# A decoder layer on one core: the MLA heads' p turned by VectorE and transfers, q, k and v of MLA ahead of both late gate groups, diff heads 5 units apart

## The chip, the core and the metric

The kernel runs on one core of a Trainium2 chip. The metric is the device time of one execution in microseconds (us). The core has TensorE (PE in the profile, with its weight loads as PEld), VectorE (DVE), ScalarE (ACT), GpSimd (POOL) and SyncE (SP). Each has an instruction queue of its own, works it off in order, and waits on semaphores for the others. Transfers between memory and the core's SBUF are issued from SP's and from POOL's queue and carried out by 16 DMA engines.

## The reference: one layer of a hybrid decoder

In float32, for 256 tokens of width 2048:

```
h = LN(ALPHA*x + 0.5*swiglu(x, ffn1));  h = LN(ALPHA*h + mixer(h));  h = LN(ALPHA*h + 0.5*swiglu(h, ffn2))
mixer(h): c_q, c_kv, k_r, dq, dk, dv, gate_mla, gate_diff = columns of h @ w_in      # 512 512 64 1024 1024 1024 2048 2048
  MLA:    q = rms(c_q) @ w_uq, k = rms(c_kv) @ w_uk, v = rms(c_kv) @ w_uv             # 8 heads, 128 + 64 rotary, v 128
          o_mla = per head: softmax(causal(q k' * scale)) v
  diff:   4 heads, two score maps each:  (softmax(s1) - lam * softmax(s2)) v, s with ALiBi and causal mask, then rms
  y = sigmoid(gate_mla) * (o_mla @ w_br_mla) + sigmoid(gate_diff) * (o_diff @ w_br_diff);  return y @ w_out
swiglu(x) = (silu(x @ w_gate) * (x @ w_up)) @ w_down                                   # d_ff 5632
```

The queries are worked in two blocks of 128 rows, the first against 128 keys, the second against 256; so a head's p is a tile of 128 x 384.

## The kernel before

**Products.** Every weight matrix product is split: both sides are taken apart into a high part (`S.copy` to float32r, an ACT cast, L154) and the rest (a DVE subtraction, L155), and three matmuls (L208, L209, L210) make one product. A weight tile of 128 x 1024 comes by a transfer from SP's queue into `raw` or `sraw`, is split into a pair of `wring` tiles (the ring has six pairs), and is used by 12 matmuls of 512 columns. One such tile with its 12 matmuls is a *unit*. The FFNs and the wide projections of the mixer go through a Strassen-like scheme with seven products and shared sums, the rest through `project`.

**Order of the work.** The program is written in the order of the units. All that isn't a weight product is hung in between by `later(n, fn)`: `fn` runs when n more units have been issued (`tick`). So the numbers given to `later` set where on each engine's queue the small work of heads, turns and transfers comes.

**Turning a row tile to columns without PE.** `turn` (L711 on) does it in four steps: DVE's STREAM_TRANSPOSE of 32 x 32 blocks into a `blocks` tile (L715), four POOL transfers of 64 KB to a `turn` buffer in memory (L717), `wait` units later one POOL transfer back into a `turned` tile (L729), and `more` units later the use: an ACT copy into column tiles (`turn_to_cols`, L737) or a split. `cols_proj` and `pair_cols` use this for qT, kT, dqT and dkT.

**Turning p on PE.** `p_cols` (L1100 on) does it for the heads' p: three PE transposes into a PSUM bank (L1103) and an ACT copy into `pt` (L1105).

**The mixer.** First the projections of the two latents, dq, dk, dv and most of the gates. Then, in `mixer`:

- four diff heads, each in four steps by `diff_head`: `scores` (matmuls L1228, then the softmax on DVE and ACT, and p = p1 - lam p2 on DVE, L1235 and L1237), `turn` (L1103, L1105), `values` (L1248 to L1250), `turn2` (four transposes of the output, L1268). Heads are 6 units apart, steps 3.
- the gate group `gate(1, 2)`, with the reads of the normed latents (`c_back`) hung into it,
- q, its rotary part, k and v of MLA from the latents,
- eight MLA heads by `mla_head`: `scores` (L1301, L1303, softmax, p scaled by its sums on DVE, L1307), `turn` (`p_cols`), `values` (L1317, L1318), 2 units apart and 2 units from step to step, hung under `gate(1, 3)` and the diff branch product,
- `gate(1, 3)`, then the branch products, where stored gates come back by POOL transfers (`get_gates`, L1332), and w_out with the second LayerNorm.

**The FFNs.** Towards the end of the gate and up products of each FFN, the turned h is fetched back in quads of 512 rows for the down product; `get_h` does it on POOL's queue (two transfers of 256 KB a quad, L893), `split_h` splits it.

**Buffers.** Small tiles come from pools with a fixed number of places: 6 for `tmp` (st, blocks, turned, qr, rope tiles and so on), 3 for p and pt, 24 for statistics; PSUM has 5 banks for weight products and 3 for the heads. A tile waits until its place's last readers are done, transfers among them.

Of the kernel before, what the change touches and what calls it, by code (L numbers as in the profile page):

```python
# [11 lines left out]
F32 = mybir.dt.float32  # L12
# [47 lines left out]
def layer_kernel(ctx: ExitStack, tc: tile.TileContext, a: dict, out: bass.AP):  # L60
# [42 lines left out]
    def later(n, fn):  # L103
        uid[0] += 1
        heapq.heappush(todo, (step[0] + n, uid[0], fn))
# [746 lines left out]
    def ffn(n, x, wgu, wdn, residual, g, bt, each, first=None, between=None, nxt=None, cols=None, norm=None, pending=None):  # L852
# [7 lines left out]
        def half(c, b, up, gate, wait=0):  # L860
            q = c // 2
            sg = tmp_tile([P, 256], "sg")
            S.activation(sg, gate, AF.Silu)
            if c % 2 == 0:
                hb[b, q] = tmp_tile([P, 512], "hb")
            o = (c % 2) * 256

            def product():
                V.tensor_tensor(out=hb[b, q][:, o:o + 256], in0=up, in1=sg, op=ALU.mult)
            if wait:  # L870
                later(wait, product)
            else:
                product()
            if c % 2 == 1:
                later(12, lambda: put_h(b, q))
# [14 lines left out]
        def get_h(q):  # L890
            raw = got[q] = act_tile([P, 2, 512], F32, "hraw")
            for b in range(2):
                nc.gpsimd.dma_start(raw[:, b, :], hT[q, b])  # L893

        def split_h(q):
            raw = got.pop(q)
# [34 lines left out]
        for p in range(1, KF // 4):  # L931
            if p == KF // 4 - 1:
                for i, q in enumerate((3, 4, 0)):
                    later(3 + 3 * i, lambda q=q: get_h(q))
                later(13, lambda: split_h(3))
                later(16, lambda: split_h(4))
            hy.group(wgu[2 * p], wgu[2 * p + 1],
                     lambda n, b, bank, snap, op, p=p: sum_done(2 * p + n, b, bank, snap, op),
                     1 < p < KF // 4 - 1, p > 1)
# [160 lines left out]
    def p_cols(p):  # L1100
# [4 lines left out]
        S.copy(pt, t[:, 0:384])  # L1105
        return pt

    def mixer(x):
        c_row = [act_tile([P, 1024], F32, "c_row") for _ in range(2)]
        kr_row = [tmp_tile([P, T], "kr_row") for _ in range(2)]  # L1110
# [41 lines left out]
        project(a["wc1"], x, KD, 256, ckv1_done)  # L1152
        project(a["wc2"], x, KD, 320, ckv2_done)

        def cols_proj(w, xx, kt, name, k0=0, more=10):
            dst = act_tile([P, 4, T], F32, name)

            def done(b, bank):
                t = tmp_tile([P, 512], name + "r")
                S.copy(t, bank)  # L1160
                later(1, lambda: turn_to_cols(t, dst, b, 4, more))
            project(w, xx, kt, 512, done, k0)
            return dst
# [3 lines left out]
        def whole(t, bank, snap, op):  # L1167
            if snap is None:
                S.copy(t, bank)
            else:  # L1170
                V.tensor_tensor(out=t, in0=bank, in1=snap, op=op)
# [13 lines left out]
        def pair_cols(w, name):  # L1185
# [10 lines left out]
        dqT = pair_cols(a["wdq"], "dqT")  # L1196
        dkT = pair_cols(a["wdk"], "dkT")
        dv = [act_tile([P, 1024], F32, "dv") for _ in range(2)]
        hy.group(a["wdv"][0], a["wdv"][1], lambda n, b, bank, snap, op: whole(
            dv[b][:, n * 512:(n + 1) * 512], bank, snap, op), False, True)  # L1200
        look(0, 0)

        back = {}

        def c_back(j):
            if j == 0:
                for key, src in turns.items():
                    back[key] = tmp_tile([P, 512], "turned")
                    nc.gpsimd.dma_start(back[key], src)
            if j >= 4:  # L1210
                i, b = divmod(j - 4, 2)
                cn.put(i, b, turned(back[i, b]))

        def gate(i, f, hook=None):
            project((a["wgm"], a["wgd"])[i][f], x, KD, 512, lambda b, bank: keep_gate(i, f, b, bank), hook=hook)

        od = Acts(MH, "od")

# [54 lines left out]

        for h in range(DH):
            for i, f in enumerate(diff_head(h)):
                later(2 + 6 * h + 3 * i + i // 3, f)
        gate(1, 2, c_back)
        qT = [cols_proj(a["wuq"][c], cn, 4, "qT") for c in range(2)]
        qrT = act_tile([P, 4, T], F32, "qrT")

        def qr_done(b, bank):
            t = tmp_tile([P, 512], "qr")
            tv = t.rearrange("p (j h i) -> p j h i", j=2, h=MH)
            rope(tv[:, 0], tv[:, 1], bank, b, MH)
            later(1, lambda: turn_to_cols(t, qrT, b, 4, 10))
        project(a["wuq"][2], cn, 4, 512, qr_done)
        kT = [cols_proj(a["wuk"][c], cn, 4, "kT", 4, 8) for c in range(2)]
        v = [act_tile([P, 1024], F32, "v") for _ in range(2)]
        for c in range(2):
            project(a["wuv"][c], cn, 4, 512, lambda b, bank, c=c: S.copy(v[b][:, c * 512:(c + 1) * 512], bank), 4)  # L1290
# [3 lines left out]
        def mla_head(h):  # L1294
# [14 lines left out]
                st["p"] = p  # L1309

            def turn():
                st["pt"] = p_cols(st["p"])

            def values():
                pt = st["pt"]
# [6 lines left out]

        for h in range(MH):
            for i, f in enumerate(mla_head(h)):
                later(8 + 2 * h + 2 * i, f)
        gates = {}

        def get_gates(f):
# [69 lines left out]
    ffn(1, xq, a["gu1"], a["dn1"], a["x"], a["ln1_g"], a["ln1_b"], keep(0), first_tokens, second_tokens, h1, a["ln1_cols"])  # L1398

    yq = mixer(h1)  # L1400
    h2 = Acts(KD, "h2", (0, 1, 2))
    ln = LayerNorm(1.0, res[0], a["ln2_g"], a["ln2_b"], keep(1), h2, a["ln2_cols"], ((1, 3, 11, 13), ()), 1,
                   (a["ln1_g"], a["ln1_b"]), (2, 7, 14, 21), lambda: yq.made[3, 1])
# [93 lines left out]
```

## Time and profile before

| what | value |
|---|---|
| time, median of 3 runs | 1973.62 us (1973.51 to 1974.14) |
| profiled execution, its own time | 1972.85 us |
| its span | 1971.1 us |
| mean granted TensorE clock | 0.998 |
| PE busy | 1955.1 us, 99% |
| DVE, ACT, POOL busy | 1773.5, 1265.5, 291.0 us |
| PE's share of the chain that ended last | 95% |
| DMA | 485.71 MB, mean 246 GB/s |

The span is the time from the first to the last instruction of the profiled execution; its own time holds what lies around it too. Busy times are sums over an engine's instructions. In a group's row stand the line, engine and operation, the names out<-in and the shapes, the count, the busy time with the mean of one in ns, and the idle time ahead with what ended it. In a timeline a PE matmul's row shows its start and its modelled length; since matmuls are pipelined, the distance of starts tells what one costs (about 0.227 us for one of 512 columns). The windows' rows give busy times and counts by engine, the granted clock, the DMA engines' share and GB/s.

### The profile page before, as it was taken

To read this page: it belongs to the slowest core of one execution; us is meant where nothing else is said; L and a number is where in the kernel's file an instruction comes from. 1 tells how busy PE (TensorE), PEld (TensorE's weight loads), DVE (VectorE), ACT (ScalarE), POOL (GpSimd) and SP (SyncE) were. 2 spreads that over 40 slices of the span, in tenths; PEclk is the share of its full clock that TensorE was granted. 3 is DMA by queue.
4 is the path that set the end of the run, shared out by engine and by line. 5 is a ranking of instruction groups with operands and counts; after the bars stand their busy time and mean duration, and the time that the engine had idled before them with its cause. 6 is when DMAs were issued, how large, how long until landed. Compare 5 with 4: busy or idle time off the path is not lost.

```text
span 1971.1 us, 25747 instructions
## 1 busy us (share of the span) xinstructions
PE 1955.1 (99%) x8784; PEld 1620.0 (82%) x8784; DVE 1773.5 (90%) x2175; ACT 1265.5 (64%) x1650; POOL 291.0 (15%) x503
## 2 busy tenths in 40 slices
PE   9999999999999999999999999999999999999997
PEld 7888888888888898888888888888888888888886
DVE  7999999999998879988976677789999999999986
ACT  6666767676655566666667765556676776665661
POOL 0112111122100010102223120001211112210000
PEclk9999999999999999999999999999999999999999
DMA  8978888777776666767667668578888878786763
GB/s 309 287 227 262 285 270 251 235 216 281 296 235 222 209 218 254 244 224 259 223 198 241 234 216 271 199 263 254 254 263 294 243 243 249 238 321 237 274 234 124
DMA packets 147478, 485.71 MB, mean 246 GB/s; under 512 B 20961, under 2 KB 21009, under 8 KB 147345
## 3 DMA queue, kind: packets, MB, share of 16 engines
q1 hardware_dynamic: 117360, 397.99, 58.2%
q0 software_dynamic: 29984, 86.07, 16.4%
q8 instruction: 69, 1.13, 0.2%
q14 instruction: 65, 0.52, 0.1%
HBM read 455.13 MB, written 28.84 MB: 246 GB/s over the span
## 4 chain that ended last, share of the span: by engine, by line
PE 95%; DVE 2%; DMA 1%; issue 1%; ACT 0%; SPq 0%; DVEq 0%; ACTq 0%
PE mm L209 30%; PE mm L210 30%; PE mm L208 30%; DVE wring L155 1%; PE tr L208 1%; PE tr L210 1%; PE tr L209 1%; DMA sraw<-in_gu_dram 1%; PE tr L671 0%; DVE sraw L428 0%; ACT wring L154 0%; DMA raw<-in_gu_dram 0%; PE tr L1228 0%; PE tr L1301 0%; PE tr L1303 0%
## 5 line engine op out<-in xcount | busy, mean ns | idle before, releaser
L154 ACT CAST wring<-raw 128x1024 fp32r<-128x1024 f32 (+2 forms) x467 | 482.2, 1038 | 296.5 <-PE mm L210 207.2
L155 DVE TENSOR_TENSOR wring<-raw,wring 128x1024 fp32r<-128x1024 f32 (+2 forms) x467 | 559.1, 1206 | 95.4 <-ACT wring L154 92.8
L154 ACT CAST wring<-sraw 128x1024 fp32r<-128x1024 f32 x436 | 454.8, 1054 | 230.2 <-DVE sraw L428 94.2
L155 DVE TENSOR_TENSOR wring<-sraw,wring 128x1024 fp32r<-128x1024 f32 x436 | 523.2, 1228 | 21.6 <-ACT wring L154 18.8
L210 PE MATMUL mm<-wring,h 128*128 128x512 f32 (+2 forms) x1248 | 480.2, 385 | 0.0
L208 PE MATMUL mm<-wring,h 128*128 128x512 f32 (+2 forms) x1248 | 480.2, 385 | 0.0
L209 PE MATMUL mm<-wring,h 128*128 128x512 f32 (+2 forms) x1248 | 479.8, 385 | 0.0
L209 PE MATMUL mm<-wring,xs 128*128 128x512 f32 x776 | 302.2, 389 | 1.3 <-DVE wring L155 1.3
L208 PE MATMUL mm<-wring,xs 128*128 128x512 f32 x776 | 302.2, 389 | 0.0
L210 PE MATMUL mm<-wring,xs 128*128 128x512 f32 x776 | 302.0, 389 | 0.0
L209 PEld LDWEIGHTS mm<-wring,h 128*128 128x128 f32 x1248 | 234.5, 188 | 46.8 <-DVE wring L155 0.7
L210 PEld LDWEIGHTS mm<-wring,h 128*128 128x128 f32 x1248 | 234.5, 188 | 46.5 <-DVE h L155 0.7
L208 PEld LDWEIGHTS mm<-wring,h 128*128 128x128 f32 x1248 | 234.4, 188 | 46.4 <-ACT h L154 0.6
L428 DVE TENSOR_TENSOR sraw<-sraw,sraw 128x1024 f32<-128x1024 f32 x168 | 200.2, 1229 | 3.5 <-DMA sraw<-in_wdv_dram 1.6
L209 PEld LDWEIGHTS mm<-wring,xs 128*128 128x128 f32 x776 | 145.7, 188 | 32.5 <-DVE wring L155 2.3
L208 PEld LDWEIGHTS mm<-wring,xs 128*128 128x128 f32 x776 | 145.7, 188 | 30.1
L210 PEld LDWEIGHTS mm<-wring,xs 128*128 128x128 f32 x776 | 145.7, 188 | 30.0
L717 POOL DMA_DIRECT2D hT<-blocks x176 | 97.1, 562 | 370.0 <-DVE blocks L715 368.2
L208 PE MATMUL mm<-wring,x 128*128 128x512 f32 x336 | 130.8, 390 | 0.8 <-ACT wring L154 0.8
L209 PE MATMUL mm<-wring,x 128*128 128x512 f32 x336 | 131.0, 390 | 0.5 <-DVE wring L155 0.5
L210 PE MATMUL mm<-wring,x 128*128 128x512 f32 x336 | 130.6, 389 | 0.0
L430 POOL DMA_DIRECT2D sraw<-in_gu_dram x40 | 35.6, 900 | 359.4 <-DVE sraw L428 309.0
(307 smaller groups left out, 2289.6 us busy)
## 6 DMA issues: line engine op xcount, KB each, us to landing
sraw<-in_gu_dram SPq DMA_DIRECT2D x160, 512.0 KB, 5.4
raw<-in_gu_dram SPq DMA_DIRECT2D x159, 512.0 KB, 4.7
raw<-in_dn_dram SPq DMA_DIRECT2D x140, 512.0 KB, 4.7
sraw<-in_gu_dram POOLq DMA_DIRECT2D x40, 512.0 KB, 6.9
sraw<-in_dn_dram SPq DMA_DIRECT2D x36, 512.0 KB, 5.6
hraw<-hT POOLq DMA_DIRECT2D x68, 256.0 KB, 6.2
eraw<-in_gu_dram SPq DMA_DIRECT2D x64, 256.0 KB, 6.0
raw<-in_w_out_dram SPq DMA_DIRECT2D x32, 512.0 KB, 4.3
```

The source lines that it names most:

```text
L154: cast[0] = S.copy(hi, src)
L155: lows[0] = V.tensor_tensor(out=lo, in0=src, in1=hi.bitcast(F32), op=ALU.subtract)
L208: PE.matmul(o, xh, wh, start=first, stop=False, skip_group_check=again)
L209: PE.matmul(o, xh, wl, start=False, stop=False, skip_group_check=again)
L210: PE.matmul(o, xl, wh, start=False, stop=last, skip_group_check=again)
L428: last = V.tensor_tensor(out=R[src][i], in0=R[src][i], in1=R[add[1]][i], op=ALU.add)
L430: nc.gpsimd.dma_start(R["12"][s], source("22", s), accum_op=ALU.add)
L717: nc.gpsimd.dma_start(to.rearrange("(g r) (i f) -> i r g f", g=4, i=4)[i], t[32 * i:32 * (i + 1), :].rearrange("r (g f) -> r g f", g=4))
```

## The change: what it does

Five edits of the program, with the same matmuls in all products:

1. `turn_p` takes the place of `p_cols` for the eight MLA heads: a DVE STREAM_TRANSPOSE of p into `pblocks`, one POOL transfer of it to memory (`pturn`), and 2 units later four POOL transfers back into `pt`, one for each 32 partitions, each of 32 x 12 pieces of 32 floats (128 bytes). `pt` now lies in the large pool. The values follow 8 units behind the scores instead of 4.
2. q, its rotary part, k and v of MLA are projected ahead of `gate(1, 2)`; both late gate groups come behind. The reads of the latents (`c_back`) are hung into the dv products instead. Uses of turned q and k come 4 units after their transfer back instead of 10 or 8.
3. Diff heads are 5 units apart instead of 6.
4. The first three quads of h in each FFN are fetched on SP's queue (`get_half`), one half at a time.
5. In the FFN the product of gate and up is written behind a split (`behind_split(3)`), and `narrow_to(6)` is called behind the mixer; neither moves an instruction.

```diff
+        def get_half(q, b):
+            if b == 0:
+                got[q] = act_tile([P, 2, 512], F32, "hraw")
+            with tc.issue_after(fetched[0].ins):
+                nc.sync.dma_start(got[q][:, b, :], hT[q, b])
...
-                    later(3 + 3 * i, lambda q=q: get_h(q))
+                    for b in range(2):
+                        later(1 + 4 * i + 2 * b, lambda q=q, b=b: get_half(q, b))
...
+    def turn_p(p, keep, more):
+
+        t = tmp_tile([P, 384], "pblocks")
+        V.transpose(t, p)
+        to = dram.tile([P, 384], F32, name=nm("pturn"))
+        nc.gpsimd.dma_start(to, t)
+
+        def back():
+            pt = act_tile([P, 384], F32, "pt")
+            for k in range(4):
+                nc.gpsimd.dma_start(pt[32 * k:32 * (k + 1), :].rearrange("f (b i c) -> f b i c", b=3, i=4),
+                                    to.rearrange("(i f) (b k c) -> k f b i c", i=4, b=3, k=4)[k])
+            keep["pt"] = pt
+        later(more, back)
...
-        def cols_proj(w, xx, kt, name, k0=0, more=10):
+        def cols_proj(w, xx, kt, name, k0=0, more=4):
...
+        back = {}
+
+        def c_back():
+            for key, src in turns.items():
+                back[key] = tmp_tile([P, 512], "turned")
+                nc.gpsimd.dma_start(back[key], src)
+        later(6, c_back)
+        for i in range(2):
+            for b in range(2):
+                later(12 + 4 * i + 2 * b, lambda i=i, b=b: cn.put(i, b, turned(back[i, b])))
...
-                later(2 + 6 * h + 3 * i + i // 3, f)
-        gate(1, 2, c_back)
+                later(2 + 5 * h + 3 * i + i // 3, f)
...
-            later(1, lambda: turn_to_cols(t, qrT, b, 4, 10))
+            later(1, lambda: turn_to_cols(t, qrT, b, 4, 4))
...
-        kT = [cols_proj(a["wuk"][c], cn, 4, "kT", 4, 8) for c in range(2)]
+        kT = [cols_proj(a["wuk"][c], cn, 4, "kT", 4, 4) for c in range(2)]
...
-                st["pt"] = p_cols(st["p"])
+                turn_p(st["p"], st, 2)
...
-                later(8 + 2 * h + 2 * i, f)
+                later(10 + 2 * h + (0, 2, 8)[i], f)
+        gate(1, 2)
```

The changed file's lines are moved: `p_cols` is L1111 and L1113 there, the MLA scores L1322 and L1324, values L1338 and L1339, the diff scores L1250 and values L1270, `pblocks` L1119, `pturn` L1121, the reads of `pt` L1126, the stored gates L1199 and L1354. Counted over the program, PE has 24 transposes less, DVE 8 instructions more, ACT 16 less (8 copies of pt and 8 table loads), POOL 28 more (8 + 32 - 12), SP 12 more.

**PE where an MLA head stands among the diff branch's matmuls.** Before, values of one head, the turn of the next, the scores of the one after (mm is a weight product's bank, tr a head's bank):

```order
4916 L210 MATMUL mm_9038<-wring_5085,od_8093 128x512
4917 L1317 MATMUL tr_9045<-pt_8981,v_8362 128x256
4918 L1318 MATMUL tr_9045<-pt_8981,v_8363 128x128
4919 L1103 MATMUL tr_9052<-ident,p_8995 128x128 x3
4920 L1301 MATMUL tr_9058<-kT_8290,qT_8031 128x128
4921 L1303 MATMUL tr_9058<-krT_5345,qrT_8103 128x128
4922 L1301 MATMUL tr_9058<-kT_8290,qT_8031 128x256
4923 L1303 MATMUL tr_9058<-krT_5345,qrT_8103 128x256
4924 L208 MATMUL mm_9014<-wring_116,od_8088 128x512
```

With the change, at the values of head 0:

```order
4804 L210 MATMUL mm_8847<-wring_104,od_8193 128x512
4805 L1338 MATMUL tr_8854<-pt_8747,v_8134 128x256
4806 L1339 MATMUL tr_8854<-pt_8747,v_8135 128x128
4807 L1322 MATMUL tr_8869<-kT_8070,qT_7824 128x128
4808 L1324 MATMUL tr_8869<-krT_5345,qrT_7877 128x128
4809 L1322 MATMUL tr_8869<-kT_8070,qT_7824 128x256
4810 L1324 MATMUL tr_8869<-krT_5345,qrT_7877 128x256
4811 L208 MATMUL mm_8821<-wring_5085,od_8188 128x512
```

The three transposes between values and scores are gone, and the scores are those of the fourth head after.

**POOL over the first MLA heads, with the change** (gates: a gate stored; pturn: a head's p to memory; pt: its reads):

```order
147 L1199 DMA gates<-gate_8559 128x512
148 L1121 DMA pturn_8660<-pblocks_8658 128x384
149 L1126 DMA pt_8747<-pturn_8660 32x12x32 x3
150 L1121 DMA pturn_8725<-pblocks_8723 128x384
151 L1126 DMA pt_8747<-pturn_8660 32x12x32
152 L1199 DMA gates<-gate_8778 128x512
153 L1126 DMA pt_8811<-pturn_8725 32x12x32 x2
154 L1121 DMA pturn_8789<-pblocks_8787 128x384
```

Before, the same stretch had the stored gates followed by their reads alone; now a head's last reads stand behind the next head's write.

**DVE at diff head 1** (st: scaled scores; nmx: the negative maxima that the exponentials need; qr the rotary part of q). Before, behind head 0's norm and output:

```order
1063 L709 SCALAR_TENSOR_TENSOR f_7941<-t_7937,y_7935 128x2
1064 L1261 SCALAR_TENSOR_TENSOR orow_7943<-tr_7919,f_7941,subg 128x256 x2
1065 L1084 SCALAR_TENSOR_TENSOR st_7949<-tr_7946,bias_92 128x384
1066 L1084 SCALAR_TENSOR_TENSOR st_7965<-tr_7962,bias_92 128x384
1067 L1086 TENSOR_REDUCE mx_7951<-st_7949 128x1
1068 L1087 TENSOR_REDUCE mx_7951<-st_7949 128x1
1069 L155 TENSOR_TENSOR wring_103<-raw_8130,wring_102 128x1024
1070 L1089 TENSOR_SCALAR nmx_7954<-mx_7951 128x2
```

With the change:

```order
1062 L155 TENSOR_TENSOR wring_115<-raw_8165,wring_114 128x1024
1063 L715 STREAM_TRANSPOSE blocks_7937<-qr_7920 128x512
1064 L1079 TENSOR_TENSOR ropec_7962<-mm_7927,sincos 128x512
1065 L1080 TENSOR_TENSOR ropes_7963<-mm_7927,sincos 128x512
1066 L1081 TENSOR_TENSOR qr_7961<-ropec_7962,ropes_7963 128x256
1067 L1082 TENSOR_TENSOR qr_7961<-ropes_7963,ropec_7962 128x256
1068 L1092 SCALAR_TENSOR_TENSOR st_7971<-tr_7968,bias_92 128x384
1069 L1092 SCALAR_TENSOR_TENSOR st_7987<-tr_7984,bias_92 128x384
1070 L1094 TENSOR_REDUCE mx_7973<-st_7971 128x1
1071 L1095 TENSOR_REDUCE mx_7973<-st_7971 128x1
1072 L715 STREAM_TRANSPOSE blocks_8009<-qr_7961 128x512
1073 L1097 TENSOR_SCALAR nmx_7976<-mx_7973 128x2
```

The rotary part of q, which came behind this head's p before, now stands ahead of its st, with one block turn, and a second block turn stands ahead of its nmx; head 0's norm comes later.

More of the change, by code (lines that the diff above doesn't have):

```diff
@@ L868, in product @@
             def product():
-                V.tensor_tensor(out=hb[b, q][:, o:o + 256], in0=up, in1=sg, op=ALU.mult)
+                with behind_split(3) if wait else nullcontext():
+                    V.tensor_tensor(out=hb[b, q][:, o:o + 256], in0=up, in1=sg, op=ALU.mult)
             if wait:
@@ L1201, in mixer, with gate @@
         look(0, 0)
[L1203 to L1215, printed above, removed]
+        def gate(i, f):
+            project((a["wgm"], a["wgd"])[i][f], x, KD, 512, lambda b, bank: keep_gate(i, f, b, bank))
         od = Acts(MH, "od")
@@ L1400, in layer_kernel @@
     yq = mixer(h1)
+    narrow_to(6)
     h2 = Acts(KD, "h2", (0, 1, 2))
```

## The prediction

> **What bounds the kernel now.** I read the page first (spans, engines, chain), then the waits of TensorE, then the chain and the timeline around the longest of these waits.
>
> ```profile
> span 1971.1 us, 25747 instructions
> PE 1955.1 (99%) x8784; PEld 1620.0 (82%) x8784; DVE 1773.5 (90%) x2175; ACT 1265.5 (64%) x1650; POOL 291.0 (15%) x503
> ...
> PE 95%; DVE 2%; DMA 1%; issue 1%; ACT 0%; SPq 0%; DVEq 0%; ACTq 0%
> ```
>
> TensorE (PE) is busy for 1955.1 of 1971.1 us and carries 95% of the chain. So the time can fall in two ways only: fewer or shorter PE instructions, or less of the 16 us in which PE does nothing. Of these 16, the waits of PE show what lies inside the run:
>
> ```profile
> engine line waited for: us in total, times, longest us
> PE mm L209 <- DVE wring L155: 1.8, 4, 0.7
> PE tr L1248 <- ACT pt L1105: 1.1, 1, 1.1
> ...
> PE mm L208 <- ACT wring L154: 0.8, 1, 0.8
> PE tr L1103 <- DVE p L1237: 0.2, 1, 0.2
> ```
>
> Only the rows of L1248 and L1103 lie in the part of the mixer that the change rewrites, 1.3 us together. The others belong to the start or to weight splits of the FFNs, whose order stays. The chain around the 1.1 us:
>
> ```profile
> 1068.04 1.05 ACT wring L154
> 1069.12 1.28 ACT L1092
> ...
> 1071.69 4.50 DMA turned<-turn
> ...
> 1076.75 1.04 ACT wring L154
> 1077.79 0.39 ACT pt L1105
> 1078.22 0.70 PE tr L1248 x2
> ```
>
> ScalarE (ACT) stood in its queue on kT, which comes back by a transfer (turned<-turn), behind a 1.28 us table load; the pt copy of the last diff head came after that, so its values (L1248) were late.
>
> **What PE loses: the turns of the MLA heads.** A stretch of PE with one head, and the start of the next:
>
> ```profile
> 1118.25 0.39 PE L210 MATMUL mm<-wring,od 128*128 128x512 f32 x1
> 1118.47 0.59 PE L1317 MATMUL tr<-pt,v 128*128 128x256 f32 x2
> ...
> 1119.12 0.49 PE L1103 MATMUL tr<-ident,p 128*128 128x128 f32 x3
> 1119.45 0.39 PE L1301 MATMUL tr<-kT,qT 128*128 128x128 f32 x2
> ...
> 1120.58 0.58 PE L208 MATMUL mm<-wring,od 128*128 128x512 f32 x1
> 1121.00 0.39 PE L209 MATMUL mm<-wring,od 128*128 128x512 f32 x1
> ...
> 1126.24 0.59 PE L1317 MATMUL tr<-pt,v 128*128 128x256 f32 x2
> ```
>
> By starts, three transposes take 1119.45 - 1119.12 = 0.33 us, and a weight matmul 1118.47 - 1118.25 = 0.22 to 0.23. Eight heads: 8 x 0.33 = 2.6 us less. Against it, the first weight matmul behind such a group takes 1121.00 - 1120.58 = 0.42, so 0.19 more than the others. Values now stand 8 units behind the scores instead of 4, and with the diff heads 5 units apart the small matmuls fall into more separate groups: in the order of the change PE goes from weight matmuls to small ones 39 times in this part, before 35 times. Four more entries at 0.11 to 0.25 (0.19 on leaving, a few hundredths on entering) give back 0.4 to 1.0. Net -1.6 to -2.2; I take -1.6, the cautious end, since with the group in another place a weight load can miss its cover too.
>
> **The waits that go.** The values of a diff head now follow its turn by 5.4 to 8 us of PE work instead of 1.6 to 3.3, and the kT transfers lie behind other work than before, so the 1.1 of L1248 and the 0.2 of L1103 go, and some 0.1 to 0.2 of restart with them: -1.5, bounds -1.0 and -1.6.
>
> **The wait that comes.** Heads closer together leave the softmax less time. In diff head 1 there were 13.7 us of PE work between the end of its scores (1008.8) and its turn, and even then p was just late:
>
> ```profile
> 1008.80 0.58 PE L208 MATMUL mm<-wring,cn 128*128 128x512 f32 x1
> ...
> 1022.14 0.39 PE L209 MATMUL mm<-wring,cn 128*128 128x512 f32 x1
> 1022.50 0.33 PE L1103 MATMUL tr<-ident,p 128*128 128x128 f32 x1
> ```
>
> (1022.50 - 1022.14 is 0.13 above 0.23.) In the change 48 PE rows, 10.9 us, stand there. VectorE (DVE) and ACT have this ahead of p:
>
> ```profile
> L155 DVE TENSOR_TENSOR wring<-raw,wring 128x1024 fp32r<-128x1024 f32 x47 | 57.3, 1221 | 18.6 <-ACT wring L154 18.0
> L715 DVE STREAM_TRANSPOSE blocks<-qr 128x512 f32<-128x512 f32 x2 | 1.4, 706 | 0.0
> L1072 DVE TENSOR_TENSOR ropes<-mm,sincos 128x512 f32<-128x512 f32 x2 | 1.4, 682 | 0.0
> L1073 DVE TENSOR_TENSOR qr<-ropec,ropes 128x256 f32<-128x256 f32 x2 | 0.8, 422 | 0.0
> L154 ACT CAST wring<-raw 128x1024 fp32r<-128x1024 f32 x46 | 48.1, 1051 | 22.3 <-PE mm L210 15.8 <-issue 5.7 <-ACT p L1093 0.8
> ```
>
> With the scores' end as 0: a weight pair ends on DVE at 1.6 (cast 1.05, subtract 1.22, begun 0.7 before), a block turn of 0.71 to 2.3, the second q rope (0.67 + 0.68 + 2 x 0.42) to 4.4 with small overlaps 4.1, then st, maxima and another block turn, to 6.5; first exponentials behind a copy, to 8.0; ACT then does a cast and a copy of q before the second ones (1.05 + 0.62), to 10.7; rs, rl and the four p operations, 1.2 until the first part: 11.9. PE wants it at 10.9. So +1.0 us, from nothing (if the cast and copy come in another overlap) to 2.0 (if the q transfer lands late, ahead of which that copy stands). I take +1.1 with the restart. Head 0 has 9.3 us but no rope in it, head 3 about 1 us of slack; nothing for these.
>
> **What the MLA turns cost elsewhere.** Per head DVE gets a block turn 128x384 (0.53 by 384/512 of 706 ns), ACT loses a copy of 0.48, POOL gets one write and four reads.
>
> ```profile
> L717 POOL DMA_DIRECT2D turn<-blocks x104 | 56.8, 554 | 168.3 <-DVE blocks L715 139.8 <-DVE ms L1126 18.4 <-DVE nmx L1089 6.7
> L747 POOL DMA_DIRECT2D cols<-in_ln_cols_dram x2 | 1.1, 548 | 0.0
> ...
> turn<-blocks POOLq DMA_DIRECT2D x104, 64.0 KB, 3.4
> turned<-turn POOLq DMA_DIRECT2D x26, 256.0 KB, 4.3
> gate<-gates POOLq DMA_DIRECT2D x16, 256.0 KB, 7.4
> ...
> cols<-in_ln_cols_dram POOLq DMA_DIRECT2D x2, 16.0 KB, 3.5
> ```
>
> From p on: 0.53 + 0.55 + landing 3.4 to 4.3 + 4 x 0.55 + landing 4.3 to 7.4 = 11 to 15 us. From scores to p a head of before had 1126.24 - 1120.58 = 5.7 us and did not wait. Sum 17 to 21. PE has 8 units of 12 matmuls, 21.8 us, and four groups of small matmuls of about 1.3 between: 23 to 27. Tightest are heads 0 and 1: POOL works in order, and their last reads stand behind the next head's write, which waits for that head's p. There the slack is 1 to 4 us, elsewhere 4 and more. So nothing on the path. POOL has 5 x 0.55 = 2.8 us of work per head, and heads come every 1126.24 - 1118.47 = 7.8 us.
>
> Unknown is the price of a read cut into 384 pieces of 128 bytes; no row has one. Below: 0.55, as for 128 pieces of 512 bytes (L717) and for 128 of 128 (L747, the nearest). Above, all of it per piece: 3 x 0.55 = 1.65, which makes the last read 4.4 us later and so eats the slack of heads 0 and 1 and up to 3.4 us more. I take 0.55, since pieces of a quarter of the size changed nothing, and +0.
>
> ```profile
> 1045.00:1066.00 21.00, 21.00 (x97) 17.56 (x96) 12.92 (x25) 15.56 (x28) 12.81 (x24) 1.00 0.83 275
> 1081.00:1101.00 20.00, 19.97 (x99) 16.19 (x98) 13.90 (x35) 13.61 (x27) 9.18 (x18) 1.00 0.81 295
> 1101.00:1142.00 41.00, 41.00 (x206) 34.83 (x205) 27.22 (x63) 36.62 (x67) 0.44 (x1) 1.00 0.49 170
> ```
>
> The DMA engines (share in the column before the last) have 0.2 to 0.5 of their time free here. 32 reads put 24 pieces on each of 16 engines, 768 per engine. At 275 GB/s and 0.83 an engine moves 20.7 bytes a ns, so 6 ns for 128 bytes, or 25 ns if a short piece costs what 512 bytes do: 5 to 19 us of engine time over some 55 us. That is free.
>
> The Trainium skill ("VectorE: DVE Perf Modes", Rules for kernel authors) says to turn 128x128 on TensorE where PSUM will do, and its section on the three transpose paths warns that a strided plain DMA is many times slower; by that rule the turns stay on TensorE and the sum is without their -1.6: -0.4. By the rows it is -2.0, since PE is the engine without spare time; no run here shows that factor.
>
> At no price: q, k, v projections and the gate group change places with the same matmuls; ACT loses 8 table loads (1.28 each), off the path; the first h quads move from POOL's queue to SP's, where no wait of PE names them now, and they wait on nothing later than their neighbours; if that cover were gone, a weight would come late by one landing, up to 6 us, in each FFN.
>
> **Sum.** -1.6 - 1.5 + 1.1 = -2.0 on a span of 1971.1; the profiled run's own time is 1972.85, so 1970.85. The median of the runs is 0.77 above that run: 1971.6 us.
>
> **Rivals.** (a) The turns go and no new wait comes: -2.6 - 1.6 = -4.2, 1969.4. For it: head 1 misses by little; against: more groups on PE. (b) The new waits are larger, head 1 at its 2.0 and heads 0 or 3 half a us, with a late pt of head 0 at 1: 1.9 more, 1973.5. (c) Slower: the 128-byte pieces fill the DMA engines. The point is where 768 pieces per engine take the 20 us that are free: 26 ns each, just above the 25 of a 512-byte piece. At 36 ns they take 28, and 8 us of weights come late, on the path: 1979.6. Against: L747's rows of 128 bytes landed in 3.5 us. The Trainium skill ("DMA: Bandwidth & Descriptors", Specifications) puts the size for full line rate at 512 bytes or more, with a read-modify-write below; no run so far shows it for reads.
>
> **Chances.** Forecast 0.44 (1970.5 to 1972.7), (a) 0.2, (b) 0.16, (c) 0.2. Within 0.2% of before, 3.95 us, which is about what a measurement of this kernel can tell from no change, lie the forecast and (b): 0.6; (a) counts as faster, 0.2; (c) as slower, 0.2. The range goes from 1968.8, (a) with the larger gain on PE, to 1979.0, in (c), of which the far end is left out.
>
> **What would show it.** PE without the L1103 group between values and scores, 24 transposes fewer; no wait of L1270 (values) for pt; a wait of about 1 us of L1111 on p near 1016; POOL's L1126 at 0.55 each and pt landing within 4 to 7 us; no wait of L1338 on pt. Wrong I am if L1338 waits for pt, if weight splits (L208, L209) wait in 1060 to 1130, or if L1126 takes over 1.5 us.

## The result and the profile after

The changed kernel takes 1968.15 us (median of 13 runs, 1967.32 to 1970.04) against 1972.58 for the kernel before in the same sets of runs (1971.91 to 1975.21): a ratio of 0.9975, 95% interval 0.9968 to 0.9983, so 3.4 to 6.3 us less. I had forecast 1971.6 in 1968.8 to 1979.0. It is faster by more than I had thought. It also lies below rival (a)'s 1969.4, but the 4.2 us of rival (a) is inside the interval. The forecast stood on 1973.62 for the kernel before, the median of the three runs that I had; in these sets the kernel before is 1.0 us lower, so a part of the distance from forecast to result is the base's.

The page of the profiled execution (1969.03 us) and the waits of PE:

```profile
span 1967.3 us, 25772 instructions
...
PE 1951.7 (99%) x8760; PEld 1618.2 (82%) x8760; DVE 1777.8 (90%) x2183; ACT 1249.7 (64%) x1634; POOL 309.3 (16%) x531
```

```profile
PE tr L671 <- DVE diff L1376: 1.8, 1, 1.8
PE tr L98 <- DVE zero L96: 1.1, 1, 1.1
PE mm L208 <- ACT snap L385: 0.6, 1, 0.6
PE mm L209 <- DVE wring L155: 0.5, 1, 0.5
PE tr L1111 <- DVE p L1259: 0.3, 1, 0.3
```

The waits of L1248 and L1103 are gone, as forecast. Of L209's four waits only the one at the start is left, which I had not forecast. Three are new: L671 (the branch output's transposes, near 1187 us), L208 on a snap copy near 958 us, and 0.3 us of L1111 at diff head 2 (1042 us). A wait for pt does not appear; the view lists waits from 0.15 us on.

Both programs have 8256 weight matmuls, so the start of the n-th can be compared. Change minus before, in us, from the two traces (in the mixer the matmuls in between stand in another order):

| n-th weight matmul | 100 | 1100 | 1300 | 4000 | 4900 | 5000 | 6400 | 6600 | last |
|---|---|---|---|---|---|---|---|---|---|
| change - before | -0.8 | -0.8 | -1.8 | -1.9 | -5.2 | -3.2 | -3.2 | -4.1 | -4.1 |

So a microsecond goes between 1100 and 1300 and again between 6400 and 6600: the same place in both FFNs. The mixer up to the last MLA head gives 3.3, and the wait of L671 takes 2.0 back in this execution. The 0.8 at the start are the first weights' arrival; there the executions differ by this much.

**The FFN place.** Before, at 237 to 258 us. First POOL, ACT and DVE in the timeline of before:

```profile
237.20 2.17 POOL L893 DMA_DIRECT2D hraw<-hT  x4 [2.13 <-DMA hT<-blocks]
...
247.38 1.05 ACT L154 CAST wring<-sraw 128x1024 fp32r<-128x1024 f32 x1 [2.71 <-DMA sraw<-in_gu_dram]
248.33 0.42 ACT L863 ACTIVATE sg<-gus 128x256 f32<-128x256 f32 x1
...
248.78 0.42 DVE L869 TENSOR_TENSOR hb<-gus,sg 128x256 f32<-128x256 f32 x1 [1.91 <-ACT sg L863]
```

Four reads of h, 1 MB, start at 237, some 145 us ahead of where they were written (in the last gate and up group, where the change reads them at 380). They run beside the weights, a weight tile lands late, ACT stands 2.71 us on it, DVE 1.91 on ACT, and ten microseconds on PE misses a weight pair. The weight's transfer takes 8.20 us in the chain, where the median of its kind is 5.4. The edit moves the split of h away from here too (1.2 us of ACT's time), but ACT stands idle behind it until the weight has landed, so the transfer is what ends last. The windows of the same stretch, before and then changed (DMA engines' share and GB/s at the end):

```profile
236.00:243.00 7.00, 7.00 (x33) 5.79 (x32) 7.00 (x9) 6.73 (x10) 2.17 (x4) 1.00 0.95 319
243.00:248.00 5.00, 5.00 (x24) 4.14 (x23) 3.87 (x5) 2.16 (x3) 0.00 (x0) 1.00 1.03 408
```

```profile
235.00:242.00 7.00, 7.00 (x33) 5.79 (x32) 7.00 (x9) 6.26 (x8) 0.00 (x0) 1.00 0.91 285
242.00:247.00 5.00, 5.00 (x24) 4.14 (x23) 5.00 (x7) 3.16 (x4) 0.00 (x0) 1.00 0.89 320
```

Before, the DMA engines are full (1.03, 408 GB/s); in the change, where the reads come at 380 to 405 us in SP's queue, they are at 0.91 and 0.89, and POOL has nothing there. POOL's order of before has it in plain sight, which I had only read for the mixer:

```order
29 L717 DMA hT_122<-blocks_1532 32x4x128 x4
30 L893 DMA hraw_3201<-hT_122 128x512 x2
31 L430 DMA sraw_462<-in_gu_dram 128x1024
...
36 L893 DMA hraw_3231<-hT_122 128x512
37 L893 DMA hraw_3282<-hT_122 128x512 x2
```

POOL's queue holds the h reads between the additions (L430) of early groups, wherever their data are there.

The profiles of the runs below bear this out, with one exception. In the nine profiles with h on SP's queue (after, again, again_2, h_sp_only, p_on_pe, heads_6, values_6, pt_twice, cn_later) no wait stands at either FFN place. In the four with h read early on POOL's queue (before, before_again, h_pool, order_only) the second FFN has a wait each time (0.36 to 0.81 us), the first in three of four: in order_only the DMA engines are as full (1.03, 393 GB/s from 243 to 248 us) and ACT stands 1.69 us on the same weight, but PE doesn't wait. In all four ACT stands idle at the first place for 1.7 to 3.5 us, against 0.9 in the change; in three of them the view names the weight's transfer, in before_again the place of the weight's pair. A microsecond or two decides whether PE feels it.

**Diff head 1**, where I had forecast a wait. DVE, ACT and PE in the timeline of the change; the scores end at 1004.23:

```profile
1010.84 0.50 ACT L1101 ACTIVATE p<-st,nmx 128x256 f32<-128x256 f32 x1
1011.33 1.04 ACT L154 CAST wring<-raw 128x1024 fp32r<-128x1024 f32 x1
1012.27 0.61 ACT L737 COPY qT<-turned 128x512 f32<-128x512 f32 x1
...
1014.74 0.74 DVE L1259 SCALAR_TENSOR_TENSOR p<-p,rs,p 128x128 f32<-128x128 f32 x2
...
1015.42 0.27 PE L1111 MATMUL tr<-ident,p 128*128 128x128 f32 x1
```

p's second part is done at 1015.48, its first some 0.35 earlier; PE comes at 1015.42. It fits, without slack.

**The reads of pt.** POOL's group and the transfers of the change:

```profile
L1126 POOL DMA_DIRECT2D pt<-pturn x32 | 21.5, 743 | 5.6 <-issue 3.1 <-DMA pturn<-pblocks 1.9 <-DMA gate<-gates 0.6
...
pturn<-pblocks POOLq DMA_DIRECT2D x8, 192.0 KB, 2.2
pt<-pturn POOLq DMA_DIRECT2D x32, 48.0 KB, 4.9
```

A read of 384 pieces takes POOL 0.74 us, between my ends of 0.55 and 1.65, and lands in 4.9 (median). From the landing of a head's last read to its values, the three profiles of the change have 1.5 to 2.3 us at head 0, 4.7 and more at heads 1 to 4, 2.3 to 3.5 at heads 5 and 6, and 0.1 to 1.7 at head 7. So the tightest head is the last, not the first two: its last read takes 7.2 to 8.8 us to land, beside the gates' reads.

### The profile page after: what moved, and what is told of

It is laid out like the page before. It is cut to its first block, busy times and chain, and to the rows that moved or that the text cites. A ratio compares the mean times of both kernels' runs of the same rounds, so it can differ in the third digit from the quotient of the medians.

```text
span 1967.3 us, 25772 instructions
## 1 busy us (share of the span) xinstructions
PE 1951.7 (99%) x8760; PEld 1618.2 (82%) x8760; DVE 1777.8 (90%) x2183; ACT 1249.7 (64%) x1634; POOL 309.3 (16%) x531
## 3 DMA queue, kind: packets, MB, share of 16 engines
q0 software_dynamic: 30560, 86.07, 16.8%
## 4 chain that ended last, share of the span: by engine, by line
PE 92%; DMA 3%; DVE 1%; issue 1%; ACT 1%; POOL 1%; SPq 0%; DVEq 0%; POOLq 0%; ACTq 0%
PE mm L209 29%; PE mm L208 29%; PE mm L210 29%; DMA turned<-turn 1%; DMA gate<-gates 1%; PE tr L210 1%; PE tr L209 1%; PE tr L208 1%; DMA turn<-blocks 0%; POOL turn L717 0%; PE tr L671 0%; ACT wring L154 0%; DMA raw<-in_wgd_dram 0%; DMA raw<-in_gu_dram 0%; PE tr L1322 0%
## 5 line engine op out<-in xcount | busy, mean ns | idle before, releaser
L208 PE MATMUL mm<-wring,h 128*128 128x512 f32 (+2 forms) x1248 | 480.9, 385 | 0.0
L209 PE MATMUL mm<-wring,h 128*128 128x512 f32 (+2 forms) x1248 | 480.0, 385 | 0.0
L208 PE MATMUL mm<-wring,xs 128*128 128x512 f32 x776 | 302.2, 389 | 0.6 <-ACT snap L385 0.6
L209 PE MATMUL mm<-wring,xs 128*128 128x512 f32 x776 | 301.9, 389 | 0.0
L208 PEld LDWEIGHTS mm<-wring,h 128*128 128x128 f32 x1248 | 234.5, 188 | 46.9 <-ACT h L154 0.6
L209 PEld LDWEIGHTS mm<-wring,h 128*128 128x128 f32 x1248 | 234.5, 188 | 46.5 <-DVE wring L155 0.4
L208 PEld LDWEIGHTS mm<-wring,xs 128*128 128x128 f32 x776 | 145.7, 188 | 31.2 <-ACT snap L385 1.0
L209 PEld LDWEIGHTS mm<-wring,xs 128*128 128x128 f32 x776 | 145.7, 188 | 30.1
L717 POOL DMA_DIRECT2D hT<-blocks x176 | 96.8, 562 | 367.0 <-DVE blocks L715 366.0
L209 PE MATMUL mm<-wring,x 128*128 128x512 f32 x336 | 130.8, 389 | 0.5 <-DVE wring L155 0.5
L208 PE MATMUL mm<-wring,x 128*128 128x512 f32 x336 | 130.8, 390 | 0.0
L430 POOL DMA_DIRECT2D sraw<-in_gu_dram x40 | 35.5, 889 | 371.3 <-DVE sraw L428 288.3
```

The source lines that it names most:

```text
L208: PE.matmul(o, xh, wh, start=first, stop=False, skip_group_check=again)
L209: PE.matmul(o, xh, wl, start=False, stop=False, skip_group_check=again)
L430: nc.gpsimd.dma_start(R["12"][s], source("22", s), accum_op=ALU.add)
L717: nc.gpsimd.dma_start(to.rearrange("(g r) (i f) -> i r g f", g=4, i=4)[i], t[32 * i:32 * (i + 1), :].rearrange("r (g f) -> r g f", g=4))
```

## The experiments

All kernels ran against the kernel before; "ratio" is to it. Where I give PE time "by kind", it is the sum of the distances from each PE start to the next, without waits, between the 4000th and the 4900th weight matmul, the stretch that holds all heads.

**again and again_2: the change itself, two more profiles.**

> The changed kernel once more, with a second profile. Theory A (systematic): the waits of L209 at the sixth weight group of both FFNs (0.73 and 0.53 us in the profile before) are absent again, the wait of L671 near 1187 us (1.8 us in the first profile of the change) is there again, ratio 0.9975. Theory B (chance): waits differ from profile to profile, and the one near 1187 us is gone or below 0.5 us.

> The changed kernel a third time, as the base of cn_later in the same set of runs: ratio 0.9975; the wait of L208 for the snap copy near 958 us (0.6 us) again; the wait of L671 near 1187 us in about half of the profiles so far.

Measured: 1968.09 (0.9976, 0.9966 to 0.9985) and 1968.51 (0.9976, 0.9966 to 0.9986). The FFN waits are absent in all three profiles of the change. L671 waits 1.8, not at all, and 0.6 us, so it comes and goes; the snap wait is there each time (0.6, 0.6, 1.1).

**before_again: the kernel before, a second profile.**

> The kernel before with a second profile. Theory A: the waits of L209 near 257 and 1531 us are there again with 0.5 to 1 us each, and the wait of L1248 for pt with 1 to 2 us; ratio 1.000. Theory B (chance): one or more of them missing.

Measured: 1.0001 (0.9992 to 1.0009). Waits of PE:

```profile
PE tr L1248 <- ACT pt L1105: 2.6, 1, 2.6
PE mm L209 <- DVE wring L155: 1.3, 3, 0.5
...
PE tr L1103 <- DVE p L1237: 0.2, 1, 0.2
```

Of L209's waits here 0.26 ends at 257.9 and 0.49 at 1532.7 us: theory A for the places, though the first was 0.73 in the other profile and is below the 0.5 that I had expected. L1248 waited 2.6 us this time. What I had read as 1.1 is a wait of 1 to 3 us.

**h_pool: the change without its fourth edit.**

```diff
-                    for b in range(2):
-                        later(1 + 4 * i + 2 * b, lambda q=q, b=b: get_half(q, b))
+                    later(3 + 3 * i, lambda q=q: get_h(q))
```

> The change without its fourth edit: h's first quads again in POOL's queue, where they stand ahead of the sixth group's and the seventh group's additions. Theory A (these reads come some 145 us early and collide with six weight tiles on the DMA engines): both FFN waits come back, near 237 to 258 us and near 1510 to 1530 us, and the time is 1.9 us above the change (1.05 + 0.85 in the comparison of the profiles). Theory B (the FFN waits of before were chance): same time as the change within 0.5 us and no such wait.

Measured: 1968.64, ratio 0.9978 (0.9969 to 0.9987); 0.55 above again, less than the runs can tell. The profile has the FFN waits at the places named:

```profile
PE mm L209 <- DVE wring L155: 2.1, 4, 1.0
```

Its matmuls lose 1.8 us against again between the 1000th and 1300th and 0.7 between the 6400th and 6600th. But this kernel has no snap wait near 958, and its heads' stretch took 234.7 us against 236.1 in again. So what the FFNs lose the mixer wins, in part. The profile bears theory A out; the time doesn't, since the 1.9 us that I expected did not come. Why the h reads of the FFN bear on the snap wait isn't settled: POOL's order there is the same row for row, but in the three profiles of the change a fourth write of a turn (L717) starts 0.97 us late, and here it doesn't. The pattern holds over the runs: with the new order of the mixer and without cn_later's edit, all seven profiles with h on SP's queue have the snap wait (0.6 to 1.2 us), and the three with h on POOL's queue (h_pool, h_pool_late, order_only) don't.

**h_sp_only: the fourth edit alone, on the kernel before.**

```diff
-                    later(3 + 3 * i, lambda q=q: get_h(q))
+                    for b in range(2):
+                        later(1 + 4 * i + 2 * b, lambda q=q, b=b: get_half(q, b))
```

> The kernel before with the fourth edit alone. Theory A: 1.9 us below before, the two FFN waits gone, the mixer as before with its waits of L1248 and L1103 (1.3 us). Theory B: same as before within 0.5 us.

Measured: 1971.23, ratio 0.9992 (0.9983 to 1.0001), 1.7 below before in the medians; no FFN wait in the profile, L1248 at 2.2 us. Theory A, by the size and by the profile; the interval takes in no change at all, so the time alone shows nothing.

**h_pool_late: POOL's queue, but late.**

```diff
-            with tc.issue_after(fetched[0].ins):
-                nc.sync.dma_start(got[q][:, b, :], hT[q, b])
+            with tc.issue_after(added[0].ins):
+                nc.gpsimd.dma_start(got[q][:, b, :], hT[q, b])
```

Here `added[0]` is the latest addition of a weight sum on POOL's queue (L430; the lines that set it are left out).

> The change with h's first quads on POOL's queue, but held behind the additions of the last group, so that they are read near 380 to 440 us as on SP's queue. If the time of the reads is the cause: no FFN waits, same as the change within 0.5 us. If POOL's queue itself is the cause (a read ahead of an addition holds it up): waits of L209 or L208 near 400 us and 1670 us, 1 to 2 us above the change.

Measured: 1973.08, ratio 1.0001 (0.9992 to 1.0010): 5 us above the change.

```profile
PE mm L209 <- DVE wring L155: 2.5, 5, 0.8
PE mm L208 <- ACT wring L154: 1.4, 2, 0.9
```

These waits stand at 385 to 387 and 1658 to 1661 us, at the last group. ACT of this run ahead of the first of them:

```profile
382.88 0.62 ACT L154 CAST h<-hraw 128x512 fp32r<-128x512 f32 x1 [5.27 <-DMA hraw<-hT]
...
384.44 0.58 ACT L386 COPY snap<-mm 128x512 f32<-128x512 f32 x1
384.91 1.05 ACT L154 CAST wring<-sraw 128x1024 fp32r<-128x1024 f32 x1
```

The reads start at 377.2, and the split of h stands in ACT's queue right behind them: ACT waits 5.27 us (4.89 in the second FFN) until h itself has landed, and the weight's cast behind it is late. In the change the first read starts at 380.0 and its split stands at 407.7, with no wait. So the edit moved the split too, and the run doesn't test POOL's queue by itself: a held-up addition is not what PE waits for here. Besides, five of the six reads start within 3 us, where SP's queue spreads them from 380 to 406. Whether the queue, the burst or the time of the reads is what did harm in the kernel before stays open. A part of the 5 us is the clock: behind the waits at 385 to 387 the granted clock is at half for 3.4 us, from 387.8 on, which is some 1.7 us of work.

**p_on_pe: the MLA heads' p turned on PE again, all else as in the change.**

```diff
-                turn_p(st["p"], st, 2)
+                t = tr_bank()
+                for i in range(3):
+                    PE.transpose(t[:, i * P:(i + 1) * P], st["p"][:, i * P:(i + 1) * P], ident)
+                st["pt"] = act_tile([P, 384], F32, "pt")
+                S.copy(st["pt"], t[:, 0:384])
```

> The change with the MLA heads' p turned on PE again (three transposes and an ACT copy at the place of the block turn), values still 8 units behind the scores, pt in the large pool. Theory A (the turns cost what PE's own intervals of the profile before show, 3.5 us for 24 transposes): 3.5 us above the change, with no wait for pt. Theory B (the cheapest rows, 0.33 us a head, hold for all): 2.0 to 2.6 us above. Theory C (the gain of the mixer is the later values and the other order alone): the same as the change within 0.5 us.

Measured: 1971.2, ratio 0.9987 (0.9979 to 0.9996), 2 to 3 us above the change. PE time by kind, in us:

| kind | before | before_again | change (again) | p_on_pe | order_only |
|---|---|---|---|---|---|
| turns of p (36, 36, 12, 36, 36) | 4.24 | 4.24 | 0.76 | 3.86 | 3.86 |
| MLA values | 5.18 | 5.18 | 4.88 | 4.87 | 4.88 |
| diff values | 5.10 | 5.10 | 4.66 | 4.67 | 4.66 |
| weight matmuls beside small ones, above 0.227 each | 4.24 | 4.16 | 4.23 | 4.44 | 4.41 |
| weight matmuls among themselves, above 0.227 | 0.39 | 0.23 | 1.33 | 1.54 | 0.59 |
| waits | 1.34 | 2.80 | 0.74 | 1.36 | 0.00 |

The turns are worth 3.1 to 3.5 us of PE: theory A by PE's time; the run's time of 2 to 3 us doesn't tell theory A from B. The weight matmuls beside small ones cost about the same (4.2 here, 4.2 to 4.6 in the three profiles of the change), though there are more groups: 28 against 22 in this stretch.

**order_only: the order of the projections and heads alone.** As p_on_pe, with the h reads of h_pool, so neither the first nor the fourth edit.

> The kernel before with the change's second and third edits and values 8 units behind, but p turned on PE and h's quads on POOL's queue. Theory A: the waits of L1248 and L1103 (1.3 us) go, the snap wait near 958 us comes (0.7 us), the FFN waits stay: 0.5 to 1 us below before. Theory B (the new order is worth most of the gain): 2 us or more below before.

Measured: 1970.77, ratio 0.9992 (0.9983 to 1.0001), 1.6 below before in the medians. No wait in the heads' stretch at all, not even the snap wait that I expected; one of 0.8 us until 1529.4. Between the theories, and the interval takes in no change: by the medians the order alone is worth about as much as the waits of L1248 and L1103.

**heads_6: diff heads 6 units apart, in the new order.**

```diff
-                later(2 + 5 * h + 3 * i + i // 3, f)
+                later(2 + 6 * h + 3 * i + i // 3, f)
```

> The change with the diff heads 6 units apart again. Theory A (nothing waits at 5): the same as the change within 0.5 us, no wait of L1111 on p either way. Theory B (5 units are too near and cost a wait of about 1 us somewhere): 0.5 to 1 us below the change. Theory C (the heads' end moves later and pushes the MLA heads): 1 us or more above.

Measured: 1969.41, ratio 0.9981 (0.9972 to 0.9990), 1 us above the change and no more than the runs can tell. But the profile has waits that none of the theories had:

```profile
PE tr L1111 <- DVE p L1259: 2.4, 1, 2.4
...
PE tr L1338 <- DMA pt<-pturn: 0.7, 1, 0.7
```

```profile
1017.54 0.71 DVE L715 STREAM_TRANSPOSE blocks<-kTr 128x512 f32<-128x512 f32 x1 [2.11 <-DMA turn<-blocks]
```

With more room between heads PE waits 2.4 us for p, until 1027.5. Ahead of that p's nmx DVE stands 2.11 us at a block turn of k, until the transfers of an earlier turn have landed. So the distance of the heads doesn't say how long a softmax has; what stands ahead of p on DVE and ACT does. The profiled execution took 1972.22, 2.8 us above this kernel's median, so it isn't shown that most executions have this wait. Behind it the granted clock is at half for 3.4 us:

```profile
1027.00:1031.00 4.00, 3.46 (x13) 3.11 (x14) 3.68 (x7) 1.99 (x6) 2.21 (x5) 0.57 0.89 248
```

(0.57 is the mean of these 4 us; weight matmuls start 0.42 to 0.43 us apart there instead of 0.227.)

**values_6: MLA values 6 units behind the scores.**

```diff
-                later(10 + 2 * h + (0, 2, 8)[i], f)
+                later(10 + 2 * h + (0, 2, 6)[i], f)
```

> The change with the MLA values 6 units behind the scores instead of 8, that is 5.4 us of matmuls less. In the profile of the change the last read of head 0 lands near 1088 with values at 1089.4, slack about 1.4 us, head 1 about 2.5. Theory A (that slack is real): PE waits for pt at head 0 by about 4 us, then little, 4 to 6 us above the change. Theory B (slack of 4 us and more, as the forecast had for most heads): 0 to 2 us above.

Measured: 1972.09, ratio 0.9995 (0.9986 to 1.0004), 4 us above the change.

```profile
PE tr L1338 <- DMA pt<-pturn: 3.9, 2, 2.0
...
PE tr L1338 <- DVE pblocks L1119: 0.8, 1, 0.8
```

PE waits 2.0 us at head 0 (until 1089.7), 0.8 at head 4 (1118.0) and 1.9 at head 6 (1134.9). By the median of the runs that is theory A's total, but not its picture: head 0 waits half as long as expected, and later heads wait too. The profiled execution, 1976.03, is the slowest of the 11. The edit also moved PE's order as a whole: counted in weight matmuls, heads 0 to 7 have 5.6, 8.2, 7.4, 5.6, 4.0, 5.4, 5.9 and 7.1 units between scores and values, where the change has 6.5 at head 0 and 8.0 at all others. So the run shows that 4 to 6 units are too few for pt, and doesn't measure the slack; the landings above do.

**pt_twice: the four reads of each pt issued twice.**

```diff
-            pt = act_tile([P, 384], F32, "pt")
-            for k in range(4):
-                nc.gpsimd.dma_start(...)
+            for _ in range(2):
+                pt = act_tile([P, 384], F32, "pt")
+                for k in range(4):
+                    nc.gpsimd.dma_start(...)
```

> The change with the four reads of each pt issued twice, first into a tile that nobody uses, then into the one that is used. POOL gets 8 x 4 x 0.74 = 24 us more and the DMA engines 768 pieces of 128 bytes more each. Theory A (POOL's queue is the limit: 2.9 us later at each head against a slack of 1.4 at head 0): waits of L1338 for pt of 1 to 2 us at the first heads and 1.5 to 4 us above the change. Theory B (the DMA engines are the limit): weights late too, waits of L208 and L209 between 1075 and 1130, 5 us or more. Theory C (both have room): the same within 0.7 us.

Measured: 1975.82, ratio 1.0012 (1.0003 to 1.0022), 7 us above the change in the medians, 5 in the profiled span.

```profile
PE tr L671 <- DVE diff L1377: 2.3, 2, 1.2
...
PE mm L209 <- DVE wring L155: 1.0, 3, 0.5
PE mm L208 <- ACT om L154: 0.7, 2, 0.4
...
PE tr L1339 <- issue: 0.6, 1, 0.6
```

```profile
L1127 POOL DMA_DIRECT2D pt<-pturn x64 | 42.8, 750 | 9.9 <-issue 3.2 <-DMA gate<-gates 2.8 <-DMA pturn<-pblocks 1.9
...
pt<-pturn POOLq DMA_DIRECT2D x64, 48.0 KB, 5.7
```

No weight is late between 1075 and 1130 us, and a read still takes 0.75 on POOL and lands in 5.7: theory B has fallen. On the page the share of POOL's transfers (q0) in the 16 engines' span goes from 16.8 to 17.2%. By that estimate the 768 more pieces per engine take some 8 us, so about 10 ns each, between my 6 and 25. The engines are not free, though: from 1105 to 1152 us their share is 0.96 to 1.04, where again has 0.69 to 0.96.

PE does wait at head 0: pt's last read lands at 1091.87, and the first matmul of the values (L1339) starts at 1091.96, 0.6 us late. That is theory A's wait, smaller than the 1 to 2 us that I had expected. The rest is not read as simply, because the edit moved PE's order as well: heads 1 to 7 have 9.6 to 12.5 units between scores and values instead of 8.0. The last heads' outputs come during the MLA branch product (its waits for om, at 1144 and 1163), and the branch output (L671) waits at 1191 and 1196. How much of the 7 us is POOL's queue, with 21 us more of work, and how much the moved order, this run doesn't separate.

**cn_later: the latents' splits hung in 2 units later.** ACT of the change (profile again) ahead of the snap wait:

```profile
949.73 0.62 ACT L154 CAST cn<-turned 128x512 fp32r<-128x512 f32 x1 [2.62 <-DMA turned<-turn]
...
958.32 0.57 ACT L385 COPY snap<-mm 128x512 f32<-128x512 f32 x1
```

```diff
-                later(12 + 4 * i + 2 * b, lambda i=i, b=b: cn.put(i, b, turned(back[i, b])))
+                later(14 + 4 * i + 2 * b, lambda i=i, b=b: cn.put(i, b, turned(back[i, b])))
```

> The change with the splits of the turned latents hung in 2 units later (14 to 20 instead of 12 to 18). Theory A (ACT stands in its queue on the latents' transfer and the snap copy of the dv products comes late): the wait of L208 near 958 us is gone, 0.6 to 0.8 us below the change. Theory B (the snap copy is late for another reason): wait and time as in the change.

Measured: 1966.53 (1965.96 to 1966.86), ratio 0.9966 (0.9953 to 0.9978), 2.0 us below again_2 of the same set. The snap wait is down to 0.05:

```profile
PE mm L209 <- DVE wring L155: 1.1, 2, 0.5
```

One of L209's waits (0.5, at 954.4) is in its place, so by the profile the gain is small at that point; its profile also has no L671 wait. Its span, 1965.1, is no shorter than that of again (1965.0), which has the snap wait of 0.6. Theory A for the wait; where the 2.0 in the medians come from stays open. It is the fastest kernel of the study, below both.

## Why the prediction was wrong

- **What bounds the kernel: right**, but I left out two rows of it. I said of the waits of L209 that they belong "to the start or to weight splits of the FFNs, whose order stays". The splits' order stays, but not the h reads beside them. This is the first step that failed. In the comparison of the n-th matmuls it is worth 1.9 us against the first profile of before and 1.4 against the second. The times of the runs say less: 1.7 in h_sp_only and 0.55 in h_pool, neither clear of no change. "The first h quads move from POOL's queue to SP's, where no wait of PE names them now" was true by the letter: the row names DVE's wring, which waited for ACT, which waited for a weight that shared the DMA engines with h. I had followed no wait back past its first releaser. The forecast had this term at nothing.
- **Turns on PE: right in kind, the term was mis-sized.** I had -1.6 net: 2.6 from the cheapest rows (0.33 us a head) less 0.4 to 1.0 for more entries. Measured: turns 4.24 to 0.76, so -3.5; values -0.3; entries +0.2. The trace has 22 groups of small matmuls in the heads' stretch before and 28 with the change, where I had counted 35 and 39. Rows such as the transposes at 1091.46 with the scores only at 1091.99 show heads that cost 0.53. One head isn't eight.
- **Waits that go: right**, -1.5 forecast; 1.3 in the profile that I had, 2.3 and 2.8 in two others of that order.
- **The wait that comes: the second step that failed.** +1.1 at diff head 1; measured 0 there, and 0, 0.1 and 0.3 at head 2. My sum of durations had the second exponentials end at 10.7 behind the scores; they ended at 1013.79, 9.6 behind. The order of the steps was as I had it, but each was earlier: the weight pair on DVE ended at 1.0 instead of 1.6, and consecutive instructions overlap (the nine DVE rows from the first block turn to nmx add up to 5.3 and took 4.7), so the first exponentials ended at 7.2 instead of 8.0. PE came at 11.2 instead of 10.9.
- **pt by transfers: right for pt, not for what stands behind it.** No wait for pt is listed; 0.74 on POOL and 4.9 landing are inside the bounds, and head 0's slack of 1.5 to 2.3 is inside my 1 to 4. But head 1 has 5.1 to 5.7, and the other tight ones are heads 5 to 7, where I had 4 and more. Rival (c) has fallen: no weight waits among the heads, and at some 10 ns a piece the 768 pieces take 8 of the 20 us that were free. But "so nothing on the path" left out the gates' reads, which stand in the same queue: the last starts at 1138 in the change, at 1099 before. The chain to L671's wait in the first profile runs over them:

```profile
1126.82 7.70 DMA gate<-gates
...
1137.72 10.01 DMA gate<-gates
...
1176.64 6.99 DMA turned<-turn
```

- **What I left out: the latents' reads in the dv products.** I didn't price the move of c_back. It brought the snap wait of 0.6 to 1.1, and cn_later takes it away; but it came only in profiles with h on SP's queue, and why is open.

The sum with measured terms, as means of the three profiles of the change against the two of before: FFNs -1.7, turns and values -3.7, diff values -0.4, waits of L1248 and L1103 -2.0, against the snap wait and slower weight matmuls +1.8, L671 +0.8 and entries +0.2: -5.0, against -4.9 by the ratio. Why the weight matmuls among themselves became slower (0.2 to 0.4 us before, 1.3 in again) isn't shown.

Of the rivals (a) came nearest, and its condition held: the turns went, and no wait came at head 1. That its -4.2 is close to the result is in part luck, for it had neither the FFNs nor the two waits that did come, and these nearly cancel.

The rule of the Trainium skill that I weighed ("VectorE: DVE Perf Modes", Rules for kernel authors: turn 128x128 on TensorE where PSUM will do) doesn't hold for this kernel: with all else as in the change, turns on TensorE took 2 to 3 us more (p_on_pe), where PE is busy for 99% of the span. The warning of the Trainium skill ("VectorE: DVE Perf Modes", The three transpose paths) that a strided plain DMA is many times slower is about a large innermost stride, and isn't put to the test here: these reads move unbroken pieces of 128 bytes, and took 0.74 us of POOL and 4.9 us to land.

## What to carry to other kernels

Follow each wait of the bounding engine back to its last releaser before calling it untouched; a row that names VectorE can end at a transfer that shares the DMA engines with something the change moves. Ask the same of a queue that gets more work: what stands behind it, and who waits for that. Look where a moved transfer stands in its own queue before, not where it is written: the h reads ran 145 us ahead of their place. And price a repeated group from all its instances, by the sum of the distances of starts, not from one clean row.

## What the runs showed that I had not expected

Reads of h on POOL's queue ran 145 us early and cost 1.4 to 1.9 us of PE's time in the profiles, while the same bytes on SP's queue, spread over 25 us among the weights, cost nothing visible there. Held back on POOL's queue they cost more, with ACT's split of h moved up behind them.

An edit of a few lines can move the built order far from it: values_6 and pt_twice changed the distance of nearly all heads on PE.

The same wait varies from execution to execution by more than I had allowed: L1248 for pt waited 1.1, 2.2 and 2.6 us in three profiles with the same mixer, L671 0, 0.6 and 1.8. And a wait can cost more than its length. In four profiles the granted clock falls to half for 3.41 us around the end of a wait or shortly behind it: h_sp_only (2.2 us at L1248), heads_6 (2.4), values_6 (1.9, at head 6) and h_pool_late (0.9 and 0.8 in quick succession). Half the clock for 3.41 us is 1.7 us of work. It doesn't follow each time: the 2.6 us of before_again and the 2.0 us of head 0 in values_6 went without. What decides it these runs don't show.
